# Shorter pinning in the first stage of a two-layer diffusion backbone, with the gate's conditioning moved together

## The chip, the cores and the metric

The kernel runs on one core of one Trainium2 chip. The metric is the device time of one execution in microseconds (us). Engines are named as in the profile: PE (TensorE), DVE (VectorE), ACT (ScalarE), POOL (GpSimd), and SP, whose queue issues the DMAs.

## What is computed

Two layers work on 512 latent and 256 context tokens of 1024 channels. Each layer has a token mixer and a squared-ReLU MLP, each between two RMS norms and with adaptive shift, scale and gate. The first stage, which the change touches, is layer 0's mixer and the way into its MLP:

```python
sh1, sc1, gt1, sh2, sc2, gt2 = ada_mods(c, w_ada[i], b_ada[i])          # silu(cond) @ w + b, split in six
csh1, csc1, cgt1, csh2, csc2, cgt2 = ada_mods(c_ctx, w_ada[i], b_ada[i])
h_lat = modulate(rms_norm(x, g_mix_pre[i]), sh1, sc1)                   # h * (1 + scale) + shift
y_lat = pool_mixer(h_lat, w_pool[j], pool_scale[j])                     # windowed mean minus identity, per-group matmul, scale
x = x + gt1 * rms_norm(y_lat, g_mix_post[i])
m_lat = sq_relu_mlp(modulate(rms_norm(x, g_mlp_pre[i]), sh2, sc2), w_mlp_in[i], w_mlp_out[i])
x = x + gt2 * rms_norm(m_lat, g_mlp_post[i])
```

The context tokens go the same way with their own conditioning. Layer 1 has grouped-query attention with rotary positions as its mixer. Weights and activations are float32.

## The kernel before

**Tiling.** The tokens are six row tiles of 128 (0 to 3 latent, 4 and 5 context), the channels eight slabs of 128. Products of the MLP and the mixer's linear map are made from a high and a low part of each operand (float32r), three matmuls for one.

**The first stage in order.** The rows of each tile are loaded (`xload`), squared and summed on ACT and turned into a reciprocal root on POOL (`rows_a`, helper `rstd`, lines 174 to 186), and scaled on DVE (`rows_b`). Band matmuls (`band_mm`) give the windowed means, in PSUM tiles `psm` (psA, latent) and `psc` (psB, context); slabs 0 to 3 are copied to SBUF (`band_ev`), slabs 4 to 7 stay in PSUM. `centred` (line 441) applies scale and shift: part 0 makes the high half of a slab on ACT, part 1 the low half on DVE from the same means. `pool_weights` (457) spreads the row `pool_scale` over the partitions with matmuls into two psB tiles, which `pool_scaled` multiplies into the mixer's weights. `pool_a` (479) is the mixer's linear map for one tile, in four groups of 256 channels with six matmuls each, 24 in all (`pspool`). Tile 4 takes two psB banks for it, the others a psA tile. `pool_ms` (493) takes the squares of its result for the norm.

**Conditioning.** The 14 pieces of layer 0 stand in `CONDITIONING` (line 36). Each is made in three steps: `ada_mm` (219) loads one or two 1 MB weight blocks (`raw`, four slots) and multiplies them into a psB tile `psada`; `ada_rows` (230) transposes it on DVE; `ada_sel` (241) turns it with small matmuls and DVE adds bias and gain (`mods`, `avec`). SC1 and SH1 are scale and shift of the mixer, GT1 its gate (in two halves of 512 channels), SC2 and SH2 those of the MLP. `gate_rows` (298) spreads a half of the gate over the partitions for each of the two streams (`ci` 0 latent, 1 context): gate columns `gc` on DVE, matmuls with the identity into a psB tile `psg`, a copy to SBUF on ACT.

**After the mixer.** `pool_b` (500) multiplies the mixer's result by the gate on DVE, in two halves, and frees its PSUM; `norm_r` (504) adds it to the rows; `norm_s` (509) takes squares on ACT and the root on POOL; `norm_c` (518) normalises, on DVE or ACT. `turn0` (374) transposes pairs of tiles into psB tiles `psx`, `mod0` (382) applies SC2 and SH2 and splits into halves, and `parts0` makes the first MLP product (`psin`, in two psA tiles, one for each half of the block).

**Memory that limits.** PSUM has two pools of four banks: psA, two tiles of two banks, and psB, four tiles of one. A tile that is written for the first time waits for a free place.

**What sets the order.** `Steps` (line 43) collects calls with a number each (`st.at`) and runs them in the order of the numbers; this is program order. The framework then schedules instructions by an estimate of its own (`schedule_with_timeline_sim`, line 40) and may put a later one first on its engine, except where an instruction is pinned behind its predecessor (`keep_in_program_order`). The class `Kept` (line 55) wraps PE with the switch `ordered`, and DVE and ACT with the switch `mixed`: while the switch is on, every instruction of the engine is pinned, and the profile shows it with line 65, the line of the wrapper. Both are switched on at 0. Before the change `mixed` goes off at 50.4 and `ordered` at 61, among the steps of lines 722 to 787. Loads of weights by SP (`raw_load`, line 121) are pinned, too. POOL is never pinned.

On PE, the steps pinned before between 48 and 61 are: turn of GT1's second half and its gate rows, SC2's first conditioning (51), mixer tile 1 (52.6), tile 2 (55.6), SH2's first conditioning (55.8), the first transposes of tiles 4 and 5 (58), mixer tile 3 (58.4), the turn of SH2 (58.6), more transposes (59.4) and the first MLP products (60.4).

Behind this stage come layer 0's MLP, layer 1's attention and layer 1's MLP, each with instructions scheduled in the same way.

Of the kernel before, what the change touches and what calls it, by code (L numbers as in the profile page):

```python
# [34 lines left out]
SH1, SC1, GT1, SH2, SC2, GT2 = range(6)  # L35
# [33 lines left out]
def backbone(ctx: ExitStack, tc, x, ctx_in, w_ada, w_pool, pool_scale, w_qkv, g_q, g_k, w_o, w_mlp_in,  # L69
             w_mlp_out, vecs, rope, band, out):  # L70
    nc = tc.nc
    ordered, mixed = [False], [False]
    sy, gp = nc.sync, nc.gpsimd
# [54 lines left out]
    def work_tile():  # L128
        return tmp.tile([P, D], F32, tag="t", name="work")

    def sm_tile(tag):
        return small.tile([P, 8], F32, tag=tag, name=tag, bufs=2 if tag == "gc" else 8)
# [69 lines left out]
    ct = ctx_in.rearrange("b (t p) d -> p (b t) d", p=P)  # L202
    xload = lambda t: sy.dma_start(xr[:, t, :], xt[:, t, :] if t < NL else ct[:, t - NL, :])
    xload(0)
    sy.dma_start(gate.rearrange("p a n -> p (a n)")[:, 8 * BW:12 * BW + 64], band)
    for t in range(1, NT):
        xload(t)
    sy.dma_start(vec, vecs[:, 0:160])
    scale_row = work_tile()[0:1]
    sy.dma_start(scale_row, pool_scale[0:1])  # L210
    one = sm_tile("sm")
    ve.memset(one, 1.0)
    sc.activation(cond[:, :, 0:2].rearrange("p k c -> p c k"), given.rearrange("p (c k) -> p c k", k=KT),
# [508 lines left out]
    st = Steps()  # L722
    for t in range(NT):
        st.at(4.6 + 1.3 * t, rows_a, t)
    landing = ((19.3, 21.4, 22.4), (23.8, 25.9, 27), (27.1, 28.15, 28.7), (28.9, 30.0, 30.5), (31.4, 32.4, 33.4),
               (33.7, 34.8, 35.2), (38.4, 40.5, 41.3), (45.2, 47.2, 48),
               (51, 53, 53.8), (55.8, 57.8, 58.6), (60.5, 61.5, 62), (62.9, 63.9, 64.4), (65.2, 66.2, 66.7), (67.7, 68.7, 69.2))
    for zs, (m, j, w) in zip(landing, CONDITIONING):
        for z, fn, also in zip(zs, (ada_mm, ada_rows, ada_sel), ((w,), (), ())):
            st.at(z, fn, 0, m, j, *also)  # L730
    st.at(0, ordered.__setitem__, 0, True)
    st.at(0, mixed.__setitem__, 0, True)
    st.at(50.4, mixed.__setitem__, 0, False)
    st.at(61, ordered.__setitem__, 0, False)
    for t, z in enumerate((7.8, 9.7, 11.2, 12.7, 14.2, 16)):
        st.at(z, rows_b, t)
    for k in (0, 2):
# [11 lines left out]
        st.at(25.8 + t / 10, band_mm, t, (4, 5))  # L749
        st.at((28.2, 30)[t - NL], band_mm, t, (6, 7))  # L750
    for k in range(KT):
        st.at([27.4, 28.8, 30.1, 31.4, 32.7, 34, 35.5, 36.8][k], centred, k, 0)
        st.at([28.6, 29.7, 31.3, 32.5, 33.8, 35.1, 36.7, 37.9][k], centred, k, 1)
    st.at(19.25, pool_weights)
    st.at(19.35, pool_load)
    for h in range(2):
        st.at((20.2, 22.1)[h], pool_scaled, h)
# [4 lines left out]
    st.at(58, lambda: split(*raws[0]))  # L762
    for h in range(2):
        for ci in range(2):
            st.at((41.9, 48.4)[h] + (0.1, 0)[ci], gate_rows, 0, GT1, ci, (h,))
    order = (4, 5, 0, 1, 2, 3)
    for z, t, g in ((30.6, 4, 0), (32.5, 4, 1), (35.4, 4, 2), (36.2, 5, 0), (36.3, 5, 1), (36.4, 5, 2), (40.4, 4, 3), (40.45, 5, 3)):
        st.at(z, pool_a, t, (g,), t == 4)
    for n, t in enumerate(order):
        b = 50.5 + 2.9 * n  # L770
        if n > 1:
            st.at((42.5, 52.6, 55.6, 58.4)[n - 2], pool_a, t)
        st.at((41.6, 42.3, 46, 55.6, 58.6, 61.4)[n], pool_ms, t)
        st.at(b, pool_b, t)
        st.at(b + 1.5, norm_r, t)
        st.at(b + 2.8, norm_s, t)
        st.at(b + 4, norm_c, t, n % 2 == 1)
# [674 lines left out]
```

## Time and profile before

| | |
|---|---|
| median of 3 runs | 1185.52 us (1184.28 to 1186.37) |
| the profiled execution | 1186.68 us, of which the span of the trace 1184.9 us |
| mean granted clock of PE | 0.991 |
| PE busy | 1146.2 us, 97% of the span |
| DVE busy | 938.6 us, 79% |
| ACT busy | 636.2 us, 54% |
| POOL busy | 67.5 us, 6% |
| DMA queue q1 | 146.32 MB, 33.9% of 16 engines' span |

The profile is that of one execution. "Busy" of PE is the time in which matmuls are in flight; the granted clock is the share of full speed that the chip gave PE. The page cuts the span into 40 equal slices and shows the busy share of each in tenths. The timeline lists instructions with start, length, engine, line, output and inputs, and in brackets the idle time before them with what ended it. DMA-issuing instructions of SP stand in it as "SPq".

### The profile page before, as it was taken

The numbers are of one execution on the slowest core, as the hardware profiler recorded it, in microseconds if no ns is written. First come the engines' busy times: TensorE is split into PE (matmuls) and PEld (weight loads), VectorE is DVE, ScalarE is ACT, GpSimd is POOL, SyncE is SP. The second block draws the span as 40 slices with busy tenths as digits, with TensorE's granted clock in tenths as the row PEclk, the third lists the DMA queues.
The fourth block names the chain that finished last, engine by engine and source line by source line (L and its number), as shares of the span: only waits on it lengthen the run. The fifth ranks groups of instructions, "written<-read, shape, count | busy, mean of one in ns | idle before, by whom it ended". The sixth has DMA issues, their size and how long they took to land. (4 is left out here: it accounts for less than half of the span.)

```text
span 1184.9 us, 15958 instructions
## 1 busy us (share of the span) xinstructions
PE 1146.2 (97%) x6172; PEld 993.3 (84%) x6172; DVE 938.6 (79%) x1538; ACT 636.2 (54%) x1080; POOL 67.5 (6%) x120
## 2 busy tenths in 40 slices
PE   6879999999999999999999999999899999999997
PEld 5568989899899988998887889998888888888886
DVE  4575867989989899897687589978587789778876
ACT  4455745544454554554576378872676346435522
POOL 2030000000000000000141210001100000000001
PEclk9889999999999999999999999999999999999999
DMA  9793203344343333233521201105234033314212
GB/s 377 290 356 128 72 36 142 147 142 142 131 155 107 142 138 139 96 127 144 205 79 38 105 1 36 37 12 207 106 139 176 30 115 140 109 36 143 107 31 111
DMA packets 25516, 147.32 MB, mean 124 GB/s; under 512 B 2785, under 2 KB 5217, under 8 KB 9698
## 3 DMA queue, kind: packets, MB, share of 16 engines
q1 hardware_dynamic: 25442, 146.32, 33.9%
q8 instruction: 48, 0.79, 0.3%
q14 instruction: 26, 0.21, 0.1%
HBM read 138.96 MB, written 7.34 MB: 123 GB/s over the span
## 5 line engine op out<-in xcount | busy, mean ns | idle before, releaser
L807 PE MATMUL pso<-units,rb 128*128 128x512 f32 x1152 | 278.3, 392 | 0.0
L807 PEld LDWEIGHTS pso<-units,rb 128*128 128x128 f32 x1152 | 214.9, 188 | 41.2
L273 DVE SCALAR_TENSOR_TENSOR rows<-raw,cond,rows 128x256 f32<-128x256 f32 x280 | 126.7, 476 | 2.0
L819 DVE TENSOR_TENSOR acc<-acc,pso 128x512 f32<-128x512 f32 x129 | 85.2, 675 | 41.6 <-PE pso L807 41.5
L562 PE MATMUL psin<-ra,rb 128*128 128x512 f32 (+1 forms) x420 | 102.2, 342 | 1.6 <-ACT ra L364 1.6
L911 PE MATMUL pso<-units,pairs 128*128 128x512 f32 x336 | 82.3, 389 | 0.0
L562 PE MATMUL psin<-ra 128*128 128x512 f32 x256 | 80.5, 389 | 0.0
L562 PEld LDWEIGHTS psin<-ra,rb 128*128 128x128 f32 x420 | 68.5, 189 | 11.8 <-ACT ra L364 1.9
L911 PEld LDWEIGHTS pso<-units,pairs 128*128 128x128 f32 x336 | 63.1, 188 | 13.1
L915 DVE TENSOR_TENSOR acc<-acc,pso 128x512 f32<-128x512 f32 x72 | 48.6, 681 | 28.7 <-PE pso L911 28.7
L183 POOL TENSOR_SCALAR ms<-ss 128x1 f32<-128x1 f32 x20 | 9.2, 462 | 1008.6 <-ACT junk L170 955.2
L686 PE MATMUL psin<-ra,units 128*128 128x384 f32 x336 | 65.5, 337 | 0.4 <-ACT psin L698 0.4
L686 PE MATMUL psin<-sums,units 128*128 128x384 f32 x336 | 63.9, 337 | 0.0
L686 PEld LDWEIGHTS psin<-ra,units 128*128 128x128 f32 x336 | 59.7, 188 | 3.9 <-ACT psin L698 0.9
L686 PEld LDWEIGHTS psin<-sums,units 128*128 128x128 f32 x336 | 58.9, 188 | 1.7
L145 DVE TENSOR_TENSOR units<-raw,units 128x1024 fp32r<-128x1024 f32 (+2 forms) x49 | 55.2, 1149 | 5.9 <-ACT units L142 5.8
L562 PEld LDWEIGHTS psin<-ra 128*128 128x128 f32 x256 | 48.1, 188 | 10.0
L142 ACT CAST units<-raw 128x1024 fp32r<-128x1024 f32 (+2 forms) x49 | 46.8, 994 | 14.3 <-PE pso L807 10.2
L817 ACT COPY acc<-pso 128x512 f32<-128x512 f32 x48 | 27.2, 588 | 48.8 <-PE pso L807 48.5
L562 PE MATMUL psin<-rb 128*128 128x512 f32 (+1 forms) x144 | 52.6, 367 | 0.2 <-DVE rb L365 0.2
L1054 PE MATMUL psq<-units,ra 128*128 128x512 f32 x216 | 51.6, 392 | 0.0
L562 PE MATMUL psin<-rb,ra 128*128 128x512 f32 x128 | 49.8, 389 | 0.0
(277 smaller groups left out, 2359.7 us busy)
## 6 DMA issues: line engine op xcount, KB each, us to landing
raw<-in_w_ada SPq DMA_DIRECT2D x48, 1024.0 KB, 5.0
raw<-in_w_mlp_in SPq DMA_DIRECT2D x32, 1024.0 KB, 4.8
raw<-in_w_mlp_out SPq DMA_DIRECT2D x32, 1024.0 KB, 5.2
raw<-in_w_qkv SPq DMA_DIRECT2D x6, 1024.0 KB, 4.9
spill<-xr SPq DMA_DIRECT2D x10, 512.0 KB, 3.2
xr<-spill SPq DMA_DIRECT2D x10, 512.0 KB, 6.7
raw<-in_w_o SPq DMA_DIRECT2D x4, 1024.0 KB, 5.0
xr<-in_x SPq DMA_DIRECT2D x4, 512.0 KB, 5.9
```

The lines of the kernel that those rows point to most:

```text
L142: a = sc.copy(hi, raw)
L145: b = ve.tensor_tensor(out=lo, in0=raw, in1=hi, op=ALU.subtract)
L183: gp.tensor_scalar(out=ms[:, 0:1], in0=ss[:, parts - 1:parts], scalar1=rest, scalar2=EPS, op0=ALU.add, op1=ALU.add)
L273: ve.scalar_tensor_tensor(out=r, in0=raw[:, k, :], scalar=cond[:, k, c:c + 1], in1=r, op0=ALU.mult, op1=ALU.add)
L562: te.matmul(ps[:, bank, o:o + ln], w[:, k, fs], rhs, start=start, stop=(k == KT - 1 and n == 2), skip_group_check=len(ks) < KT)
L686: te.matmul(bank, w[k], a[k], start=start and k == 0 and m == 0, stop=stop and k == 3 and m == 2, skip_group_check=True)
L807: te.matmul(pss[h][:, 0:cols[h][1]], a[:, f, ts_], w[:, f, cols[h][0]:sum(cols[h])], start=(n == 0 and not seeded[t]), stop=(n == len(seq) ...
L817: sc.copy(d, ps)
L819: ve.tensor_tensor(out=d, in0=d, in1=ps[:, 0:w], op=ALU.add)
L911: te.matmul(ps, a, w, start=(m == 0), stop=(m == len(seq) - 1))
L915: ve.tensor_tensor(out=M[n][:, t], in0=M[n][:, t], in1=ps, op=ALU.add)
L1054: te.matmul(ps, a[:, k, sl], w[:, k % 4, :], start=(k == 0 and n == 0), stop=(k == KT - 1 and n == 2))
```

## The change

The change edits only numbers and order in the first stage:

- `pool_weights` runs at 7 instead of 19.25, and the load of its row is issued right behind the first row tile, ahead of the band, the other row tiles and `vec`.
- The high halves of slabs 4 and 5 stand together, and those of 6 and 7; the low halves follow.
- GT1's second half is conditioned right behind its first (44.2), ahead of mixer tile 0, the third in the order; gate rows of both halves (46.2 and 47.6) come ahead of that tile, too (47.9). Squares of tiles 4 and 5 come ahead of the gate rows.
- `mixed` goes off at 47.3 and `ordered` at 48. The steps behind that keep their numbers, but for the squares of tile 0 (46 to 50.6).

```diff
     xload(0)
+    scale_row = work_tile()[0:1]
+    sy.dma_start(scale_row, pool_scale[0:1])
     sy.dma_start(gate.rearrange("p a n -> p (a n)")[:, 8 * BW:12 * BW + 64], band)
     for t in range(1, NT):
         xload(t)
     sy.dma_start(vec, vecs[:, 0:160])
-    scale_row = work_tile()[0:1]
-    sy.dma_start(scale_row, pool_scale[0:1])
...
-               (33.7, 34.8, 35.2), (38.4, 40.5, 41.3), (45.2, 47.2, 48),
+               (33.7, 34.8, 35.2), (40.6, 42.65, 43.9), (44.2, 46.25, 47.2),
...
-    st.at(50.4, mixed.__setitem__, 0, False)
-    st.at(61, ordered.__setitem__, 0, False)
+    st.at(47.3, mixed.__setitem__, 0, False)
+    st.at(48, ordered.__setitem__, 0, False)
...
-        st.at([27.4, 28.8, 30.1, 31.4, 32.7, 34, 35.5, 36.8][k], centred, k, 0)
-        st.at([28.6, 29.7, 31.3, 32.5, 33.8, 35.1, 36.7, 37.9][k], centred, k, 1)
-    st.at(19.25, pool_weights)
+        st.at([27.4, 28.8, 30.1, 31.4, 32.7, 32.8, 35.5, 35.6][k], centred, k, 0)
+        st.at([28.6, 29.7, 31.3, 32.5, 34, 35.15, 36.7, 37.9][k], centred, k, 1)
+    st.at(7, pool_weights)
...
-            st.at((41.9, 48.4)[h] + (0.1, 0)[ci], gate_rows, 0, GT1, ci, (h,))
+            st.at((46.2, 47.6)[h] + (0.1, 0)[ci], gate_rows, 0, GT1, ci, (h,))
     order = (4, 5, 0, 1, 2, 3)
-    for z, t, g in ((30.6, 4, 0), (32.5, 4, 1), (35.4, 4, 2), (36.2, 5, 0), (36.3, 5, 1), (36.4, 5, 2), (40.4, 4, 3), (40.45, 5, 3)):
+    for z, t, g in ((30.6, 4, 0), (32.5, 4, 1), (35.4, 4, 2), (36.2, 5, 0), (36.3, 5, 1), (36.4, 5, 2), (42.6, 4, 3), (42.62, 5, 3)):
         st.at(z, pool_a, t, (g,), t == 4)
...
-            st.at((42.5, 52.6, 55.6, 58.4)[n - 2], pool_a, t)
-        st.at((41.6, 42.3, 46, 55.6, 58.6, 61.4)[n], pool_ms, t)
+            st.at((47.9, 52.6, 55.6, 58.4)[n - 2], pool_a, t)
+        st.at((43.8, 44.6, 50.6, 55.6, 58.6, 61.4)[n], pool_ms, t)
```

## The prediction

> **What bounds the kernel now.** I read the page's 40 slices first. TensorE (PE) is 97% busy over the span, so a microsecond counts only where PE stands still or is clocked down, and the slices show that only at the very start.
>
> ```profile
> PE   6879999999999999999999999999899999999997
> PEclk9889999999999999999999999999999999999999
> ```
>
> Each digit is a slice of 29.6 us: the first three hold the thin part, and the clock is short in slices 2 and 3. The change touches just this stretch. The page's chain that ended last is of little use here, since 32% of it is "issue"; so I cut 35 to 91 us into windows (busy us with counts for PE, PEld, DVE, ACT, POOL; then granted clock, DMA share, GB/s).
>
> ```profile
> 35.00:40.00 5.00, 3.27 (x50) 1.69 (x42) 3.73 (x10) 1.55 (x3) 0.00 (x0) 0.98 1.01 411
> 40.00:46.00 6.00, 5.10 (x24) 5.11 (x24) 3.35 (x8) 3.17 (x7) 0.00 (x0) 0.50 0.71 292
> 60.00:75.00 15.00, 11.86 (x102) 8.39 (x102) 13.37 (x17) 9.36 (x17) 5.55 (x8) 0.96 0.94 376
> 70.00:75.00 5.00, 1.86 (x18) 0.53 (x10) 4.90 (x5) 3.44 (x8) 3.59 (x4) 0.89 0.80 275
> 75.00:80.00 5.00, 5.00 (x25) 5.00 (x25) 1.95 (x2) 0.74 (x2) 0.79 (x2) 0.50 0.99 329
> 80.00:85.00 5.00, 1.76 (x17) 1.28 (x16) 2.85 (x6) 4.09 (x10) 1.46 (x4) 0.84 0.96 389
> 85.00:91.00 6.00, 5.02 (x29) 3.23 (x29) 2.75 (x4) 4.54 (x7) 3.37 (x5) 0.50 0.80 278
> ```
>
> Three stretches run at half clock, and two of them follow holes in PE. Then I followed PE alone through the timeline (start, length, what, and in brackets the idle time before it with its releaser).
>
> ```profile
> 49.91 0.25 PE L65 MATMUL psada<-work,sel 128*32 128x8 f32 x8
> 50.74 2.02 PE L65 MATMUL psg<-ident,gc 128*128 128x128 f32 x16 [0.57 <-DVE gc L65]
> ...
> 55.55 1.92 PE L65 MATMUL psada<-raw,cond 128*32 128x512 f32 x16
> ...
> 59.28 2.05 PE L65 MATMUL psg<-ident,gc 128*128 128x128 f32 x16 [0.48 <-DVE gc L65]
> ...
> 63.12 3.14 PE L65 MATMUL pspool<-rb,ra 128*128 128x256 f32 x24
> ...
> 74.76 0.90 PE L65 MATMUL psx<-ident,acc 128*128 128x128 f32 x3 [3.14 <-ACT acc L521]
> 75.31 5.47 PE L65 MATMUL pspool<-rb,ra 128*128 128x256 f32 x24
> 80.71 0.25 PE L65 MATMUL psada<-work,sel 128*32 128x8 f32 x8
> ...
> 84.79 0.58 PE L65 MATMUL psin<-ra,rb 128*128 128x256 f32 x1 [3.24 <-ACT ra L395]
> 86.36 2.72 PE L65 MATMUL psin<-ra,rb 128*128 128x256 f32 x11 [0.98 <-DVE ra L396]
> ```
>
> "L65" marks an instruction that went through the pinning wrapper. PE is pinned up to the first product (psin), and both long waits are those of a pinned queue. From 71.62 to 74.76 it stands before the transposes of tiles 4 and 5 (psx), which wait for tile 5's normalised rows, while the last mixer tile (pspool, 75.31) is queued behind. That tile's 24 matmuls then take 5.47 us, against 3.14 for the tile at 63.12. And the transposed conditioning of SH2 (psada, 80.71) stands behind that tile, so the first modulated block is late again: 3.24 and 0.98 us.
>
> **The change, part by part.** *Gate, as the sum's first term.* The same PE instructions are put in another order: after the turn of GT1's first half (ends 50.16) now come its second half's 16 matmuls (1.92, to 52.08), gate rows of half 0, the turn, gate rows of half 1, and only then mixer tile 0, third in the order. The weights for GT1's second half keep their place in SP's queue; both loads are in by then, since the DMA engines are only 0.71 busy from 40 to 46 us: their queue ran empty. The 0.57 us that PE waited for the gate columns is now covered by these 16 matmuls.
>
> ```profile
> 51.91 0.59 ACT L65 COPY gate<-psg 128x512 f32<-128x512 f32 x1 [1.85 <-PE psg L65]
> ```
>
> Something is added. psB has four banks; tile 4 holds two, GT1's two halves the others. So the gate rows of the second stream, 1.02 us (half of 2.02), wait until the bank of the first stream's rows is copied out: 0.59 us and the way there and back, 0.70 together. Behind them PE holds the turn, half 1 and tile 0; the vector engine's gate columns wait for the turn.
>
> Step by step: 52.08, plus 1.02, 0.70, 1.02, turn 0.25, columns 0.48, half 1 2.05, tile 0 3.14 gives 60.7. Before, the same work was done at 61.33 (59.28 + 2.05). **Gain 0.7**; without the bank wait it would be 1.4, and -0.3 if half 1's two streams wait for a bank too. More important: with the same copies of 0.59, the second gate half reaches SBUF at 57.1 and 58.2 instead of 60.9 and 61.9, so the chains of tiles 4 and 5 start 3.8 us earlier.
>
> For the second term, the rows of a tile's norm chain:
>
> ```profile
> 69.48 1.05 ACT L170 ACTIVATE junk<-xr 128x1024 bf16<-128x1024 f32 x1
> ...
> 70.71 1.27 POOL L177 TENSOR_SCALAR ms<-ss 128x1 f32<-128x1 f32 x1 [1.88 <-ACT junk L170]
> 72.06 1.46 POOL L185 TENSOR_TENSOR rs<-ms,nhalf 128x1 f32<-128x1 f32 x1
> 75.84 0.22 POOL L177 TENSOR_SCALAR ms<-ss 128x1 f32<-128x1 f32 x1 [1.27 <-ACT junk L170]
> 76.14 0.57 POOL L185 TENSOR_TENSOR rs<-ms,nhalf 128x1 f32<-128x1 f32 x1
> 89.94 1.15 ACT L521 ACTIVATE acc<-xr,rs 128x1024 f32<-128x1024 f32 x1 [0.99 <-POOL rs L185]
> ```
>
> *PE unpinned from the gate on, the second term.* The scheduler then puts an instruction where its inputs are ready by its own estimate. Tile 5's chain gives the earliest time for psx: gate product done at 58.8, two residuals of 1.27 to 61.4, squares 1.25 (1.05 and their readout), statistic 1.1, normalising 1.15: 65, or 66 to 67 if another tile's squares come between, before the last mixer tile's turn. So the hole of 3.14 goes in either order of the two, with 5.47 - 3.14 = 2.33 of slow clock. The SH2 turn no longer stands behind tile 3, so 3.24 + 0.98 go, with half of the 5.02 busy us at clock 0.50 from 85 to 91, 2.5. Together 3.14 + 2.33 + 3.24 + 0.98 + 2.5 = **12.2 at most**.
>
> What is late next is the vector engine: busy 13.37 of 15 us from 60 to 75. From the gate on it owes the last tile the first four of these groups (57 to 92 us; busy, mean ns), plus some 2 for the transposes and sums of two conditionings.
>
> ```profile
> L329 DVE SCALAR_TENSOR_TENSOR xr<-acc,rs,xr 128x1024 f32<-128x1024 f32 x6 | 7.6, 1271 | 0.0
> L326 DVE TENSOR_TENSOR acc<-pspool,gate 128x512 f32<-128x512 f32 x10 | 6.5, 682 | 4.7 <-ACT gate L65 1.8 <-ACT junk L65 1.8 <-ACT junk L170 1.1
> L145 DVE TENSOR_TENSOR rb<-raw,rb 128x2048 fp32r<-128x2048 f32 x1 | 2.3, 2292 | 0.4 <-ACT rb L142 0.4
> L523 DVE TENSOR_SCALAR acc<-xr,rs 128x1024 f32<-128x1024 f32 x3 | 2.3, 751 | 2.6 <-POOL rs L185 2.6
> ...
> L396 DVE TENSOR_TENSOR ra<-acc,ra 128x512 fp32r<-128x512 f32 x2 | 1.4, 688 | 0.0
> L391 DVE TENSOR_SCALAR acc<-psx,avec,mods 128x256 f32<-128x256 f32 x2 | 1.0, 533 | 0.0
> ```
>
> 7.6 + 6.5 + 2.3 + 2.3 + 2.0 = 20.7 from 57.4 on: 78.1. Then squares 1.25, statistic 0.8 to 2.7, normalising 1.15: tile 3 is ready at 81.3 to 83.2 if nothing else is slipped in. Four blocks of modulation ahead of it, 0.53 + 0.69 each on this engine, make it 86 to 88. Before, it was ready at 91.1 (89.94 + 1.15). So the last tile gains 3 to 9.8. PE has other work until then (conditioning, transposes, products of the first four tiles), but that needs the same vector engine. I give back 3.7 us of new PE waits and, as they come close together, one more slow stretch of 2.3: 6.0. The bounds are 0 and 11.
>
> ```profile
> 38.05 1.07 PE L65 MATMUL psada<-raw,cond 128*32 128x256 f32 x16 [0.28 <-DVE mods L65]
> ...
> 40.90 5.49 PE L65 MATMUL pspool<-rb,ra 128*128 128x256 f32 x24 [0.96 <-DVE ra L65]
> ```
>
> [...] Here PE's single waits were 0.28 to 0.96 us, and the clock was 0.50 from 40 to 46 nevertheless. [...]
>
> ```profile
> 38.89 0.78 ACT L65 ACTIVATE ra<-psm,phase,avec 128x512 fp32r<-128x512 f32 x1 [3.45 <-DVE ra L65]
> 44.22 0.48 DVE L65 SCALAR_TENSOR_TENSOR ra<-psc,avec,ra 128x256 fp32r<-128x256 f32 x1
> ```
>
> *High halves in pairs.* ACT's high half of slab 5 waited for the vector engine to finish the low half of slab 4 out of the same PSUM tile; that wait goes. Slab 5's low half still stands behind a transpose of PE's matmuls at 38.05 (to 39.12, and some 0.5 for the transpose), so it gains 0.1 at most. For slabs 6 and 7, the low half of 6 now waits for both high halves: the last low half ends between 0.5 earlier and 0.7 later than 44.70. Its reader, the last group of tiles 4 and 5, comes behind the slow 5.49 us and 2 us of conditioning, at 48.3: 2.9 us of cover, **cost nothing**; at full clock the cover would be 0.6.
>
> ```profile
> 5.07 0.33 SPq L210 DMA_DIRECT2D work<-in_pool_scale  x1
> ...
> 18.51 1.98 PE L65 MATMUL psg<-work,sm 1*128 1x512 f32 x4
> 26.53 1.06 PE L65 MATMUL psada<-raw,cond 128*32 128x512 f32 x8 [0.71 <-DMA raw<-in_w_ada]
> ```
>
> *Pool weights and scale.* PE's four matmuls of the scale row leave 18.51 for PE's idle start, ahead of the first tile's band. The 1.98 us are worth nothing, since PE waits for weights at 26.53 and the DMA engines are still full from 35 to 40. SP's issue of the scale (0.33) now stands ahead of the band and five row tiles: a cost of 0 to 0.33; I take 0.2.
>
> **Sum.** 0.7 + 12.2 - 6.0 - 0.2 = 6.7, rounded to 7. The profiled execution took 1186.68 (span 1184.9, 1.8 around it), 1.16 over the median; 7 off it is 1179.7, and off the median of 1185.52, **1178.5**. Its own range, with 3.2 to 7.7 given back, is 1176 to 1180.5.
>
> ```profile
> raw<-in_w_ada SPq DMA_DIRECT2D x48, 1024.0 KB, 5.0
> ```
>
> **Rivals.** (1) *All is recovered*: PE never lacks work, as after 91 us now. 9.5 to 13 off: 1172.5 to 1176, mean 1174. Against it is the vector engine's 89% load. (2) *The last tile's chain takes over.* The statistic on POOL took 1.27 + 1.46 beside long vector instructions and 0.22 + 0.57 without; if the denser vector engine makes each one of the slow kind and modulation blocks go first, the last tile gains 3: 1182.5 (1180.5 to 1184). [...] (3) *The order does not change*: the scheduler's estimate gives the order that was pinned; the gate's 0.7 stays: 1184.8. (4) *Slower: PE waits for conditioning weights.* Unpinned, the four last loads' matmuls (SC2, SH2) may be placed as soon as the scheduler believes the weights there. A load lands 5.0 us after its issue, which waits for a slot. One such wait with the slow clock after it costs up to 5.0 + 2.3 = 7.3, two 14.6: 1178.5 + 14.6 = 1193. It decides from 9.4 us of such waits on (7 + 2.4). For it: at 26.53 PE waited for such a load even in a pinned order. Against it: the DMA engines have gaps (0.71 busy from 40 to 46, 0.80 from 70 to 75).
>
> **Chances.** Forecast 0.45; (1) 0.13; (2) 0.22; (3) 0.07; (4) 0.13. About 0.2%, 2.4 us, is what can be told from no change: faster 0.45 + 0.13 + two thirds of (2) = 0.73; same, the rest of (2) and (3), 0.14; slower 0.13. The range of 1173.5 to 1187 leaves out (4) and the far third of (1).
>
> **What would show it.** Right: no PE wait over 2 us and clock 1.00 from 60 to 75 us; gate copies done by 58.5; last mixer tile in about 3.1 us, ending near 74; ACT's or the vector engine's normalising of the last tile between 82 and 88. Half clock from 40 to 46 as before. Wrong: PE waits "<-DMA raw" after 60; a wait of 3 us before psx; a product (psin) ahead of the last mixer tile that takes its psA slot; or a loss behind 120 us, where the order was free before as well.

## The result and the profile after

The changed kernel takes **1178.47 us** in the median (1176.59 to 1180.48), the kernel before, measured beside it, 1184.38 (1182.49 to 1187.33). The ratio is 0.9948, with an interval of 0.9933 to 0.9964: half a per cent faster. The profiled execution of the changed kernel took 1178.11 us, with a span of 1176.3 and a mean granted clock of 0.996, against 0.991 in the profile of before.

The windows of the first stage after the change, with the columns of the prediction's window rows:

```profile
40.00:46.00 6.00, 5.13 (x43) 3.58 (x43) 3.26 (x9) 2.93 (x6) 0.00 (x0) 1.00 0.79 329
60.00:75.00 15.00, 14.63 (x136) 10.76 (x134) 12.43 (x19) 9.43 (x19) 7.50 (x11) 1.00 0.73 284
75.00:80.00 5.00, 2.38 (x28) 1.33 (x29) 4.21 (x10) 4.97 (x11) 2.82 (x6) 0.90 0.91 305
80.00:85.00 5.00, 5.00 (x41) 3.61 (x41) 4.08 (x8) 4.99 (x9) 0.79 (x2) 0.76 1.02 415
85.00:91.00 6.00, 6.00 (x63) 5.10 (x63) 2.21 (x7) 1.18 (x2) 0.00 (x0) 1.00 1.02 414
```

PE is busy for 14.63 of the 15 us from 60 to 75, where it was 11.86. What is left of the thin part lies from 75 to 80 us, with a reduced clock into the next window. From 40 to 46 us the clock is 1.00 where it was 0.50. The timeline of PE after the change:

```profile
40.88 3.10 PE L65 MATMUL pspool<-rb,ra 128*128 128x256 f32 x24 [0.87 <-DVE mods L65]
43.90 1.92 PE L65 MATMUL psada<-raw,cond 128*32 128x512 f32 x16
...
49.29 1.16 PE L65 MATMUL psg<-ident,gc 128*128 128x128 f32 x8
51.13 1.16 PE L65 MATMUL psg<-ident,gc 128*128 128x128 f32 x8 [0.68 <-ACT gate L65]
...
52.95 2.05 PE L65 MATMUL psg<-ident,gc 128*128 128x128 f32 x16 [0.48 <-DVE gc L292]
54.76 3.11 PE L65 MATMUL pspool<-rb,ra 128*128 128x256 f32 x24
57.80 1.92 PE L227 MATMUL psada<-raw,cond 128*32 128x512 f32 x16
...
62.71 1.04 PE L227 MATMUL psada<-raw,cond 128*32 128x512 f32 x2
...
67.12 1.92 PE L227 MATMUL psada<-raw,cond 128*32 128x512 f32 x14
...
73.20 0.60 PE L490 MATMUL pspool<-rb,ra 128*128 128x256 f32 x3
...
75.05 1.07 PE L227 MATMUL psada<-raw,cond 128*32 128x256 f32 x16 [0.42 <-DVE mods L249]
...
77.57 0.33 PE L379 MATMUL psx<-ident,acc 128*128 128x128 f32 x1 [1.19 <-DVE acc L391]
...
79.52 1.54 PE L379 MATMUL psx<-ident,acc 128*128 128x128 f32 x6 [1.35 <-ACT acc L521]
80.99 1.73 PE L227 MATMUL psada<-raw,cond 128*32 128x256 f32 x16
```

From 57.80 on the lines are the instructions' own (227, 490, 379) and no longer 65: PE is free there. Conditioning, mixer tiles and transposes take turns, and the last three matmuls of the last mixer tile even stand behind transposes (73.20). The waits of 3.14, 3.24 and 0.98 us are gone; 0.42, 1.19 and 1.35 have come. The free order has a price of its own, too: two of 16 conditioning matmuls run ahead alone and take 1.04 us (62.71), and the other 14 take 1.92 (67.12), as long as 16 take together (57.80). That is about 1.0 us more.

To see how early the stage is left, I take the first matmul of the MLP's second product in the same view, in before and after:

```profile
132.20 4.96 PE L807 MATMUL pso<-units,rb 128*128 128x512 f32 x21
```

```profile
122.03 5.64 PE L807 MATMUL pso<-units,rb 128*128 128x512 f32 x24
```

That is 10.17 us earlier, more than the 8.6 between the spans (1184.9 - 1176.3). The difference is given back around 845 us. There the same product (psin) runs behind the same waits in both kernels, first before, then after:

```profile
851.67 0.50 PE L562 MATMUL psin<-ra,rb 128*128 128x256 f32 x2 [1.64 <-ACT ra L364]
...
854.05 0.40 PE L562 MATMUL psin<-ra,rb 128*128 128x256 f32 x2
```

```profile
841.57 0.50 PE L562 MATMUL psin<-ra,rb 128*128 128x256 f32 x2 [1.64 <-ACT ra L364]
...
844.24 0.63 PE L562 MATMUL psin<-ra,rb 128*128 128x256 f32 x2
```

The same instructions, 0.40 in one execution, at a granted clock of 1.00 (from 846 to 862 us), and 0.63 in the other, at 0.50 (from 843.55 to 846.96 us): the clock, not a wait. The second profile of the changed kernel does not have this stretch, so the spans of two profiles can't be subtracted without looking for them.

### The profile page after: what moved, and what is told of

It is laid out like the page before. It is cut to its first block, busy times and chain, and to the rows that moved or that the text cites. A ratio compares the mean times of both kernels' runs of the same rounds, so it can differ in the third digit from the quotient of the medians.

```text
span 1176.3 us, 15958 instructions
## 1 busy us (share of the span) xinstructions
PE 1145.3 (97%) x6172; PEld 989.6 (84%) x6172; DVE 938.4 (80%) x1538; ACT 635.0 (54%) x1080; POOL 68.1 (6%) x120
## 5 line engine op out<-in xcount | busy, mean ns | idle before, releaser
L562 PEld LDWEIGHTS psin<-ra,rb 128*128 128x128 f32 x432 | 70.9, 193 | 11.0 <-ACT ra L364 1.9
```

The lines of the kernel that those rows point to most:

```text
L562: te.matmul(ps[:, bank, o:o + ln], w[:, k, fs], rhs, start=start, stop=(k == KT - 1 and n == 2), skip_group_check=len(ks) < KT)
```

## The experiments

Theory A: the freed PE queue makes the gain. Rival B: the gate's order makes it, since the chains of tiles 4 and 5 start earlier. Rival C: the early scale row makes it, through the clock from 40 to 46 us. The times of before are those measured beside each kernel. They differ from one group of runs to the next (medians of 1182.92 to 1185.21), so kernels of different groups are compared by their ratios.

### PE freed, nothing else

The kernel before with one number changed:

```diff
-    st.at(61, ordered.__setitem__, 0, False)
+    st.at(50.4, ordered.__setitem__, 0, False)
```

> The kernel before with one edit: PE's pins end at 50.4, with those of the two other engines, instead of 61; gate, halves and scale row stay as before. Theory A (the freed PE queue makes the gain): the two waits of 3.1 and 3.2 us go and the last mixer tile takes 3.1 us; 4 to 6 us faster than before, 1179 to 1180.5. Theory B (the earlier second gate half makes it, by the chains of tiles 4 and 5): the gate rows of half 1 still end at about 61.3 us, tile 5's rows are normalised at about 73, and PE waits for them wherever they stand; 0 to 1.5 us faster, 1183 to 1184.5.

Measured: 1179.01 us (1176.74 to 1180.64) against 1185.21 (1182.63 to 1186.96), ratio 0.9948 (0.9934 to 0.9963), the ratio of the whole change. PE's timeline of this kernel:

```profile
40.48 5.49 PE L65 MATMUL pspool<-rb,ra 128*128 128x256 f32 x24 [0.92 <-DVE ra L65]
...
78.05 1.07 PE L227 MATMUL psada<-raw,cond 128*32 128x256 f32 x16 [1.22 <-DVE mods L249]
...
81.24 1.76 PE L379 MATMUL psx<-ident,acc 128*128 128x128 f32 x7 [1.25 <-ACT acc L521]
...
125.16 5.64 PE L807 MATMUL pso<-units,rb 128*128 128x512 f32 x24
```

The long holes are gone with this one number: PE is busy for 14.98 of the 15 us from 60 to 75. The tile at 40.48 is slow in this profile (granted clock 0.50 from 40 to 46 us); without the 2.4 us that this costs (5.49 - 3.10), the MLP's second product would start at 122.8 by estimate, within 0.8 of the whole change.

### Gate order without the earlier release

The changed kernel, with the pins held as long as before:

```diff
-    st.at(47.3, mixed.__setitem__, 0, False)
-    st.at(48, ordered.__setitem__, 0, False)
+    st.at(50.4, mixed.__setitem__, 0, False)
+    st.at(61, ordered.__setitem__, 0, False)
```

> The changed kernel with the pins of before: DVE and ACT to 50.4, PE to 61. Theory A: the order of the last mixer tile, the transposes and SH2's turn is pinned again; the turn still stands behind the last mixer tile, so a wait of 2 to 3 us and a slow stretch remain there; 1 to 3 us faster than before. Theory B: nearly the whole gain, 5 to 6 us, 1178 to 1179.5.

Measured: 1183.71 us (1181.81 to 1187.97), ratio 0.999 (0.9979 to 1.0002): no difference that can be told. The waits of PE from 60 to 95 us (in total, times, longest):

```profile
PE psin L65 <- ACT ra L395: 6.7, 1, 6.7
PE psx L65 <- DVE acc L326: 2.6, 1, 2.6
```

Before, the holes at this place were 3.14, 3.24 and 0.98, 7.36 in all; here they are 9.3. What the gate's order wins, the pinned queue loses again in front of the first product. B falls. Theory A left this kernel 1 to 3 us; the medians give 1.5, and the interval of the ratio does not tell it from nothing. With PE free, the gate's order, the pairs and the early row together show at most the 0.8 us above, and nothing in the ratio.

### Centred slabs in the old order

The changed kernel, with the old numbers of `centred`:

```diff
-        st.at([27.4, 28.8, 30.1, 31.4, 32.7, 32.8, 35.5, 35.6][k], centred, k, 0)
-        st.at([28.6, 29.7, 31.3, 32.5, 34, 35.15, 36.7, 37.9][k], centred, k, 1)
+        st.at([27.4, 28.8, 30.1, 31.4, 32.7, 34, 35.5, 36.8][k], centred, k, 0)
+        st.at([28.6, 29.7, 31.3, 32.5, 33.8, 35.1, 36.7, 37.9][k], centred, k, 1)
```

> The changed kernel with the high halves of slabs 5 and 7 each behind the low half of the slab before, as in the kernel before. If the pairs are hidden behind PE's queue, as the prediction had it: the time of the changed kernel within 1 us, and the low half of slab 5 ends at most 0.1 us later. If the pairs carry a part of the gain: 1 us or more slower than the changed kernel.

Measured: 1178.93 us (1178.43 to 1180.93), ratio 0.9951 (0.9936 to 0.9965). The group of mixer matmuls that starts at 40.88 in the changed kernel starts at 41.15 here. The pairs are worth 0.3 us at that place, and nothing that the time shows.

### Scale row at its old place

The changed kernel, with the scale's load and `pool_weights` where they were:

```diff
     xload(0)
-    scale_row = work_tile()[0:1]
-    sy.dma_start(scale_row, pool_scale[0:1])
...
     sy.dma_start(vec, vecs[:, 0:160])
+    scale_row = work_tile()[0:1]
+    sy.dma_start(scale_row, pool_scale[0:1])
...
-    st.at(7, pool_weights)
+    st.at(19.25, pool_weights)
```

> The changed kernel with the scale row and its four matmuls where they were before. If PE's conditioning between 24 and 32 us is bound by the landing of the weights: the first matmuls of SH1's second load start within 0.3 us of 26.6, and the time is that of the changed kernel within 1 us. Theory C (the early matmuls keep PE's clock up, so that the slow stretch of 40 to 46 us goes): the slow stretch is back, 2.4 us slower than the changed kernel.

Measured: 1177.37 us (1176.33 to 1178.17), ratio 0.9936 (0.9922 to 0.995). The clock from 40 to 46 us is 1.00 in its profile, too. C falls: the early row does not bring the gain. The median is 1.1 us below the changed kernel's, a little outside the 1 us expected, so the early row may cost that much; the intervals of the two ratios overlap and can't tell it from nothing.

### Normalising on one engine

These two ask which engine is late next, the vector engine as the prediction had it, or ACT. The changed kernel alternates `norm_c` between them; first all of it on DVE, then all on ACT.

```diff
-        st.at(b + 4, norm_c, t, n % 2 == 1)
+        st.at(b + 4, norm_c, t, False)
```

> The changed kernel with all six tiles' normalising (norm_c) on the vector engine: takes 3 x 1.15 us from ACT and adds 3 x 0.75 us to DVE. In the changed kernel's trace both are nearly full from 75 to 85 us (ACT 9.96 of 10, DVE 8.29). If the vector engine is what is late next, as the prediction had it: PE's waits before the first products grow by up to 2 us, 0 to 2 us slower than the changed kernel. If ACT is: the waits of 1.4 and 1.2 us before the transposes shrink, 1 to 2.5 us faster, 1176 to 1177.5.

> The opposite: all six on ACT, adds 3 x 1.15 us to ACT and takes 3 x 0.75 us from DVE. If the vector engine is late next: 0 to 2 us faster than the changed kernel. If ACT is: 1 to 3 us slower, with PE's waits there longer by as much.

Measured: 1179.17 us (1176.31 to 1181.65), ratio 0.9965 (0.9952 to 0.9978) with all on DVE, and 1179.44 (1178.85 to 1181.54), ratio 0.9971 (0.996 to 0.9982) with all on ACT, both against 1182.92. The window from 75 to 85 us, in the changed kernel, with all on DVE, and with all on ACT:

```profile
75.00:85.00 10.00, 7.38 (x68) 4.94 (x69) 8.29 (x17) 9.95 (x19) 3.60 (x8) 0.83 0.97 360
```

```profile
75.00:85.00 10.00, 7.24 (x67) 4.90 (x68) 9.21 (x19) 7.95 (x15) 4.35 (x8) 0.83 1.01 367
```

```profile
75.00:85.00 10.00, 6.00 (x49) 3.61 (x38) 5.57 (x11) 9.94 (x19) 3.23 (x8) 0.72 1.01 366
```

In the changed kernel ACT is full (9.95 of 10) and DVE has room (8.29). Two us taken from ACT bring nothing, as DVE then fills to 9.21 and PE waits for DVE's normalising instead (1.5 us, from its list of waits); the MLP's second product starts at 121.89, as good as unchanged. Adding to ACT costs: PE is busy for 6.00 instead of 7.38, and that product starts at 125.18 instead of 122.03. PE's longest wait there, 2.6 us, ends with a transpose on DVE, which itself stood behind 1.8 us of waiting for ACT's squares. So it is the two engines together, with ACT the fuller one: the 1 to 2.5 us that a relief of ACT was expected to bring if ACT alone were late did not come. The intervals of the ratios overlap and say no more.

### Matmuls in the waits

The changed kernel, with 12 matmuls of tile 4's first group put into two waits of PE:

```diff
+    st.at(32.45, pool_a, 4, (0,), True)
+    st.at(35.39, pool_a, 4, (0,), True)
```

> The changed kernel with twelve added matmuls, 2 x 0.98 us: the first group of tile 4's linear map is made twice more, with the same result, in PE's waits of 0.8 and 0.9 us ahead of 37.3 and 40.9 us. Of the changed kernel's runs, three of seven had a granted clock of 0.993 to 0.994 and took 1180.4 us, the others 0.996 to 0.997 and 1176.6 to 1178.5. If the slow stretch from 40 to 46 us comes from PE's low load in the 4 us ahead, and whether it comes depends on where the clock's observation falls: no run under 0.995 and none over 1179.5, median 1177 to 1178. If the load ahead has nothing to do with it: again both kinds of runs, and 0 to 1 us slower for the added work.

Measured: 1176.79 us (1176.29 to 1179.26), ratio 0.9955 (0.9942 to 0.9968), with a granted clock of 0.996 to 0.998 in all executions. That fits the expectation's first case, with a median 0.2 below its range; by its ratio the kernel is not faster than the changed kernel's 0.9948, since before ran at 1182.92 beside it. Next, the same with the scale row at its old place, and the changed kernel once more on the same chip:

> The changed kernel with two things together: the 12 filler matmuls of the run before (tile 4's group 0 is multiplied three times, the last result counts) and the scale row and pool weights at their old place. If the two small gains seen singly are real and add, the median lies near 1175.5, that is 2 to 3 below the changed kernel in the same call. If they are only the scatter of the granted clock from execution to execution, it lies within 1.5 of the changed kernel in this call, with a clock of 0.994 to 0.998.

> The changed kernel once more, for the comparison on one chip. Median 1176.5 to 1179.5, ratio to the kernel before 0.993 to 0.997. If the half clock at 40 to 46 us is chance, it may stand in this profile though the first profile of the changed kernel lacks it; if order removes it, it is absent again.

Measured: both edits together 1176.29 us (1175.02 to 1176.87), the changed kernel 1178.06 (1176.62 to 1180.16), the kernel before 1185.14 (1182.25 to 1187.49). The ratios to before are 0.9925 (0.9912 to 0.9939) and 0.9944 (0.9928 to 0.9961). The clock from 40 to 46 us is 1.00 again in the second profile of the changed kernel. Both edits together are the fastest version of all, 1.8 us below the changed kernel: less than the 2 to 3 expected of a sum, a little more than the 1.5 of pure scatter, with the two ranges overlapping by a quarter of a us. Its window and its start of the second product:

```profile
75.00:85.00 10.00, 8.10 (x87) 5.85 (x88) 7.83 (x17) 8.62 (x15) 2.79 (x6) 1.00 0.99 360
```

```profile
120.45 5.64 PE L809 MATMUL pso<-units,rb 128*128 128x512 f32 x24
```

The clock stays at 1.00 from 75 to 85 us, where it is 0.83 in both profiles of the changed kernel. The same stretch is at 1.00 with the extra matmuls alone, too. They stand 40 us earlier and fill none of the waits from 75 to 85 us; what differs there is that the scheduler has moved the work of ACT (8.62 for 9.95) and shortened PE's waits from 2.96 to 2.42 us. That these shorter waits keep the clock up fits the busy shares in the last section, but no run changes them alone.

### The kernel before with the same matmuls, and again

The edit is the one above, in the kernel before; and the kernel before without any edit, for a second profile.

> The kernel before, pinned as it was, with the same 12 filler matmuls between 33 and 41 us and nothing else. Theory, waits and clock each make half of the change's gain: only the stretch at 40 to 46 goes to full clock (2.5 us at most, and less in the mean, since many executions do not have it), and the waits of 3.1 and 3.2 us from 71 to 85 with the slow clock behind them stay; 1181 to 1184, 0.5 to 2 below the kernel before. Rival, the clock in the early waits is what the change gains by: nearly all of the 6 us, 1178 to 1179.5.

> The kernel before, one more profile of it. If the half clock at 40 to 46 belongs to its order, it is there again; if it is chance, it may be gone. The holes of about 3.1 and 3.2 us at 71 and 81 us and the half clock behind each are there in any case.

Measured: 1182.43 us (1180.38 to 1182.72) with the matmuls, ratio 0.9971 (0.996 to 0.9983). That lies within the theory's 1181 to 1184, though 2.7 below before and not 0.5 to 2, and far from its rival's 1178 to 1179.5. PE's timeline in the second profile of before:

```profile
40.70 3.13 PE L65 MATMUL pspool<-rb,ra 128*128 128x256 f32 x24 [0.96 <-DVE ra L65]
...
72.08 0.55 PE L65 MATMUL psx<-ident,acc 128*128 128x128 f32 x3 [3.15 <-ACT acc L521]
72.38 4.61 PE L65 MATMUL pspool<-rb,ra 128*128 128x256 f32 x24
...
81.00 0.58 PE L65 MATMUL psin<-ra,rb 128*128 128x256 f32 x1 [3.25 <-ACT ra L395]
82.57 2.71 PE L65 MATMUL psin<-ra,rb 128*128 128x256 f32 x11 [0.99 <-DVE ra L396]
...
89.73 1.09 PE L379 MATMUL psx<-ident,acc 128*128 128x128 f32 x8
...
128.30 5.64 PE L807 MATMUL pso<-units,rb 128*128 128x512 f32 x24
```

Behind the same wait of 0.96 the tile at 40.70 takes 3.13 us, at a granted clock of 1.00 from 40 to 46 us; in the first profile of the same kernel it took 5.49, at 0.50. So the half clock from 40 to 46 us isn't a property of the kernel's order, and the 2.4 us that it costs are no part of the change. The holes are there to a hundredth: 3.15, 3.25, 0.99. Against this profile the MLP's second product starts 6.3 us earlier after the change (128.30 - 122.03), in line with the medians (5.9 to 7.1 us apart). PE's idle time from 33 to 91 us gives most of it; before again, then after:

```profile
sum 58.00, PE 45.72 PEld 33.88 DVE 34.65 ACT 30.44 POOL 13.47; mean PE 6.53 PEld 4.84 DVE 4.95 ACT 4.35 POOL 1.92
```

```profile
sum 58.00, PE 51.25 PEld 36.87 DVE 39.24 ACT 33.56 POOL 13.25; mean PE 7.32 PEld 5.27 DVE 5.61 ACT 4.79 POOL 1.89
```

51.25 - 45.72 = 5.5 us less idle. The slower clock of before adds to that. By estimate it costs about 4 us in before's second profile (the tile at 72.38 in 4.61 us for 3.13, the 12 product matmuls from 81.00 on in 0.58 + 2.71 for the 1.70 of the next 12, and 16 conditioning matmuls in 1.88 for 1.07), against 1.4 after the change (worked out below). Idle and clock together make about 8, which is more than the 6.3: the free order gives some of it back, about 1.0 by the two matmuls at 62.71, and 0.7 stay open. In that comparison waits and clock are not halves, as the expectation above put it: the waits carry about two thirds, and the slow clock stands right behind them.

With the matmuls in the kernel before, the two holes are 0.8 and 6.7 us by its list of waits, 7.5 in all against 7.4, and the order stays pinned. With the early waits filled the clock is 1.00 from 40 to 46 us, as it is in the second profile of before without that, but nothing is taken off the holes; of these runs only those with the freed queue do.

## Why the prediction was right, point by point

**The sum, and luck.** The gain measured beside the kernel before is 5.9 us (1184.38 to 1178.47), and 7.1 in the second comparison (1185.14 to 1178.06), for a forecast of 7. That 1178.5 was met to the hundredths is luck: the 1185.52 from which the forecast counted down was 1.1 above the median of before that stands beside the result. The clock terms, 2.33 and 2.5, were also read from an execution with more half clock than another of the same kernel, as the last section shows.

**What bounds.** Right: two holes of a pinned PE queue. Freeing the queue alone gives the ratio of the whole change, and holding it gives none.

**Gate.** Forecast a gain of 0.7, with a bank wait of 0.70 and a columns wait of 0.48. Measured 0.68 and 0.48. From the start of GT1's first half to the end of this work it takes 13.97 us (43.90 to 54.76 + 3.11) and took 15.02, by the first of these rows of before and the 61.33 of the prediction:

```profile
46.31 2.05 PE L65 MATMUL psada<-raw,cond 128*32 128x512 f32 x16
...
58.55 0.25 PE L65 MATMUL psada<-work,sel 128*32 128x8 f32 x8 [1.07 <-DVE work L65]
```

That is 1.05. Of the difference to 0.7, 0.13 are the slow first group of before (2.05 for 1.92). The copies of the gate's second half end at 54.7 and 55.6, some 2.5 us earlier than forecast, of which 2.4 are those of the clock from 40 to 46. ACT's timeline of the changed kernel, with the last tile's normalising in its last row:

```profile
54.14 0.58 ACT L305 COPY gate<-psg 128x512 f32<-128x512 f32 x1 [1.24 <-PE psg L65]
55.04 0.59 ACT L305 COPY gate<-psg 128x512 f32<-128x512 f32 x1 [0.31 <-PE psg L65]
...
82.35 1.14 ACT L521 ACTIVATE acc<-xr,rs 128x1024 f32<-128x1024 f32 x1
```

**PE freed.** Forecast 12.2 at most, 6.0 given back, net 6.2. Measured behind the gate: 10.17 - (61.33 - 57.87) = 6.7. The three waits, the slow mixer tile and the slow clock from 85 to 91 went as listed. The last mixer tile ends at 73.8 (forecast near 74), the last tile is normalised from 82.35 on (forecast 82 to 88), and PE waits for no weights after 60 us.

**Given back: the mechanism held, the engine and the sizes did not quite.** Forecast were 3.7 us of new waits and 2.3 of slow clock; measured are 0.42 + 1.19 + 1.35 = 2.96 and about 1.4 of clock. (The 1.4: six transposes in 1.54 us where eight take 1.09 at 89.73 of before's second profile, so 0.72 over, and 16 matmuls in 1.73 where they take 1.07, so 0.66 over.) **The weak step is "what is late next is the vector engine".** From 75 to 85 us ACT is busy for 9.95 of 10 us and DVE for 8.29; the longest new wait is for ACT. The prediction summed DVE's debt and put nothing of the kind beside it for ACT, which owes squares, normalising and the halves of the modulation at the same time. That the sums came out near each other is in part luck, helped by both engines being close to full there.

The terms add up to 1.05 + 12.2 - 4.4 - 0.2 = 8.7, and the stage shows 10.17 - 2.4 = 7.8. Some 0.4 of the difference is the price of the half clock: the mixer tile took 5.47 us for 3.14 in it, 1.74 times as long and not twice, so the 5.02 us at this clock lose 2.1 and not 2.5. The two conditioning matmuls that ran ahead alone cost about 1.0, a term that the prediction did not have; it is more than the other 0.5.

**Pairs.** Forecast to be hidden, with 0.6 us of cover at full clock. The old order gives the same time. In the changed kernel the last low half of DVE runs from 44.69 for 0.47, and its reader on PE, the last group of tiles 4 and 5, starts at 45.76, 0.60 us behind it.

**Scale row.** Forecast a cost of 0 to 0.33, since PE then waits for weights anyway. After the change PE's row for this wait is:

```profile
26.68 1.06 PE L65 MATMUL psada<-raw,cond 128*32 128x512 f32 x8 [1.16 <-DMA raw<-in_w_ada]
```

It started at 26.53 behind a wait of 0.71: with the 1.98 us out of its way it waits 0.45 longer, and it starts 0.15 later. Right, though the late row's median of 1.1 us less leaves a larger cost possible.

**Half clock from 40 to 46 as before.** Wrong, and in an instructive way: the trace of one execution was read as a property of the order. It was absent after the change, present when PE alone is freed, and absent in the second profile of before. The last section has the two profiles of before side by side.

**The clock behind short waits.** The prediction read from its trace that the clock was at half behind single waits of no more than 0.96 us, and gave 2.3 us back to one more slow stretch. It was well that it did: the clock fell to 0.50 again at 78.97 us, among waits of 0.42, 1.19 and 1.35 us, and about 1.4 us were lost there.

**Rivals.** All recovered (1174): refuted by the 2.96 us of new waits in the profile; even the lowest time is 1176.59. The last tile's chain (1182.5): POOL's slow statistic did occur in the changed kernel, as these rows of POOL show, but not for the last tile, which had 0.22 and 0.57:

```profile
66.06 1.81 POOL L183 TENSOR_SCALAR ms<-ss 128x1 f32<-128x1 f32 x1 [4.52 <-ACT junk L170]
...
72.67 1.46 POOL L185 TENSOR_TENSOR rs<-ms,nhalf 128x1 f32<-128x1 f32 x1
...
81.11 0.22 POOL L177 TENSOR_SCALAR ms<-ss 128x1 f32<-128x1 f32 x1 [1.34 <-ACT junk L170]
81.42 0.57 POOL L185 TENSOR_TENSOR rs<-ms,nhalf 128x1 f32<-128x1 f32 x1
```

Unchanged order (1184.8): that is about what holding the pins gives, 1183.71, but the scheduler did choose another order. Waits for conditioning weights (1193): none after 60 us.

## What to carry to other kernels

When an engine is 97% busy and its queue is pinned, find the pinned instruction that waits longest and see what stands ready behind it: here 7.4 us of holes shrank to 3 by releasing the queue earlier, while a better order inside the pinned stretch gained nothing. When such a hole closes, sum the debt of every engine that feeds it, not only of the one that looks busiest, as the next bound here was two nearly full engines together. When the queue is freed, look also whether groups that ran together are broken up. Before a stretch of low clock is counted as a term, look whether a second profile of the same kernel has it.

## What the runs showed of the hardware

**The half clock came in stretches of 3.41 us or two or three times that, and where they lay differed from one execution to the next.** In the trace of before the stretches with a granted clock of 0.50, ahead of the last 2 us, begin at 39.81, 73.94 and 84.18 us and last 6.83 us each; their starts are 34.13 and 10.24 us apart, ten and three times 3.41. In that of the changed kernel they begin at 78.97 and 843.55 us and last 3.41 each. From 33 to 91 us the clocks of the other eleven profiles add up to stretches of about 3.4, 6.8 or, in the kernel before with the extra matmuls, 10.2 us; two of them, those with the extra matmuls in the changed kernel, have none there. In the second profile of before the stretches begin near 73.2 and 80.1 us. These rows are cut into pieces of 3.41 us, or twice that, which fit the starts of each profile's slow stretches, first in the profile of before, then in the second profile of the same kernel, with the columns of the prediction's window rows:

```profile
36.39:39.80 3.41, 1.74 (x33) 0.87 (x33) 2.63 (x8) 0.91 (x2) 0.00 (x0) 1.00 1.01 411
39.81:46.63 6.82, 5.86 (x36) 5.43 (x38) 3.54 (x8) 3.36 (x7) 0.00 (x0) 0.50 0.65 267
```

```profile
35.70:39.11 3.41, 2.12 (x30) 1.05 (x28) 2.69 (x8) 0.42 (x1) 0.00 (x0) 1.00 1.01 411
39.12:42.53 3.41, 2.08 (x23) 1.99 (x24) 2.46 (x7) 2.04 (x4) 0.00 (x0) 1.00 1.01 423
```

PE has the same waits in both, to a hundredth. In the first, most of them fall into one piece, in which PE is busy for 1.74 of 3.41 us (0.51), and 6.82 us at half clock follow. In the second they are shared by two pieces (0.62 and 0.61), and the clock stays up. So one kernel had the tile at 40 us in 5.49 or in 3.13 us. In the 3.41 us ahead of the five slow stretches named above PE was busy for 0.51, 0.32 and 0.23 in before, and for 0.41 and 0.51 in the changed kernel. The share alone does not decide, though: 0.47 from 836.72 to 840.13 us in the changed kernel, and 0.53 and 0.52 from 845.35 to 852.17 us in before, were not followed by half clock. What else decides is not shown by these runs.

**These stretches go with the scatter of the times.** The profile of before that the prediction read has six times 3.41 us at half clock in its first 100 us, the second one three times, those of the changed kernel once each. By estimate 3.41 us at half clock in which PE is fully busy cost 1.5 us (3.41 - 3.41 / 1.74) and 0.0014 of the mean clock. The 14 executions of before that were measured last run from 1182.25 us at a mean clock of 0.996 to 1187.49 at 0.990, so 0.001 of mean clock is about 0.9 us, near that estimate. Around 844 us (from 843.6 to 847.0) one such stretch made a pair of matmuls take 0.63 for 0.40; the second profile of the changed kernel does not have it (mean clock from 600 to 850 us 1.00, against 0.99 in the first).

**A few extra matmuls in waits of under 1 us seem to hold the clock up.** With 12 of them the changed kernel ran at 0.996 to 0.999 in all ten executions, while four of its own twelve were at 0.994 or below. The kernel before, with them, ran at 0.993 to 0.996 in ten, where half of the 14 without were at 0.992 or below. The late scale row alone had five of five at 0.996 or above, too, so a part of this may be the luck of few executions. The busy shares fit it: from 33 to 46 us PE is idle for 1.01, 1.09 and 1.13 us in the three profiles with the extra matmuls, so it is busy for at least 0.67 of any 3.41 us there; in the profiles of before and after without them some 3.41 us there have as little as 0.47 and 0.49.
